# Sums of squares per tile on TensorE, the second memory kept in DRAM as two halves, one attention as a background job, longer lags in the odd layer

## The chip, the cores and the metric

The kernel is one program on one core of a Trainium2 chip. The metric is the device time of a launch in microseconds (us), lower is better. Almost all data is fp32; the large matrix products run on fp32r pairs (a value is kept as hi plus lo, and three products hi·hi, hi·lo, lo·hi are added).

## The reference, cut to what matters

One inference step of a two-layer decoder trunk, for 1024 prompt tokens and 8 sample tokens that share all weights.

```
for layer in (0, 1):
    mkv = rms_norm(mem_prompt, mem_norm[layer]) @ w_mem_kv[layer]      # memory keys and values, 256 rows
    h   = rms_norm(x, norm_pre[layer])
    mix = even_mixer(h, mkv, ...) if layer == 0 else odd_mixer(h, mkv, ...)
    x   = x + rms_norm(mix @ w_out, norm_post[layer])

def rms_norm(x, g):        return x * rsqrt(mean(x * x, -1) + EPS) * g
def memory_attend(q, kv):  p = softmax(q @ k * MEM_HD**-0.5);  return p @ v          # 4 heads
# even_mixer: gated DeltaNet (4 heads), dilated sliding-window attention (3 groups x 4 heads), memory attention (4 heads)
# odd_mixer : RG-LRU (8 tiles of 128 channels, in 4 blocks), memory attention (4 heads)
```

The sample tokens attend to cached keys and values instead, and the caches are copied out, shifted by one position.

## The kernel before, in words

Channels lie on the 128 partitions and tokens along the free axis, in three chunks of 352, 336 and 344 columns (the last 8 columns are the sample tokens). A projection (`proj`, `mm3`) makes one 128-channel tile: it loads 128 weight columns into one of 3 buffers (tag "w"), ScalarE casts them to hi, GpSimd takes lo (line 154), and TensorE runs 24 products for each chunk into one PSUM bank of the pool "p"; a drain on ScalarE or VectorE empties the bank. After each chunk `tick()` moves background jobs on by one step. A job is a generator in a named lane ("group", "combine", "cached", "norm0" ...); `yield n` makes it skip n-1 ticks. What a tick issues is placed behind the last instruction that each engine has so far. A planner then orders all instructions by simulated readiness, so the order on an engine is fixed when the program is built, and an engine that meets an instruction whose input is late waits.

Tiles of one tag share that tag's buffers. In the pool "me" the tags "qm", "gm" and "mm" have one buffer each: `mem_head` keeps a query in "qm", a gate in "gm" and the mix in "mm", and `swa_ahead` (line 517) takes the three in turn for projections that it makes ahead of their use.

The stages that the change touches, in order of time:

- Start (0 to 80 us). `mem_norm` and `x_rstd` call `chan_rstd` (209): 8 squares on ScalarE, VectorE adds each odd square to the even one before it (215), and `tok_rstd` (188) sums the four results over channels with matmuls against a column of ones (197), one group of accumulating products for each block of 128 tokens; then rsqrt on [128 x 3] values and a product that spreads the result. `mem_kv(0)` projects the first memory meanwhile.
- The DeltaNet stage around 290 to 370 us. VectorE inverts 32x32 triangles in a serial loop (746, 748) at high priority; `mem_head(0)` and three `swa_ahead` projections (keys (0,), (0,1,0), (0,0,0), in tiles pa0, pa010, pa000) fill TensorE. `mem_scaled` (295) multiplies the memory by its norm factors on GpSimd (302) and stores 1 MB to `memd` (303) on ScalarE's DMA queue.
- The end of the even layer (1075 to 1180 us). Head 3: `swa_gate(3)` (tile wb3), `mem_query` (wq03), `mem_gate` (wg03), then `mem_attend` (356) for head 3, then `mix_put` (1358) splits the 12 mix tiles into hi and lo for the output projection (tiles wo00, wo01 ...); the tile of head 7 comes from the job `combine` (1041), the tile 11 from the attention.
- Between the layers (1270 to 1400 us). `chain` (1442) normalises the output (po), adds the residual and calls `chan_rstd` for the next layer's norm (pr); `mem_reload` (305) loads `memd` through the "w" buffers and splits it (278 on ScalarE, 279 on VectorE) into the tags mb; `mem_kv(1)` projects it (mk10 to mv13).
- The odd layer (1400 to 1760 us). Projections, `recur` (the scan of the RG-LRU, mostly VectorE and ScalarE) and one job `mem_cached` for each head in the lane "cached". Such a job has two tiny matmuls on TensorE: mx (421) transposes a maximum, VectorE makes a row of it (423 to 427), my (430) spreads that row.

Of the kernel before, what the change touches and what calls it, by code (L numbers as in the profile page):

```python
# [15 lines left out]
P = 128  # L16
# [49 lines left out]
def body(ctx, tc, I, O):  # L66
# [34 lines left out]
    def ptile(name):  # L101
        return banks["a"].tile([P, 512], F32, name=name, tag="a")
# [85 lines left out]
    def tok_rstd(pool, sqs, n, scale, name, pt=None):  # L188

        nb = -(-n // P)  # L190
        pt = pt or ctile
        cols = pt(f"{name}c")
        x, y, t = (pool.tile([P, nb], F32, name=f"{name}{i}", tag=f"tr{i}{nb}", bufs=2) for i in "xyt")
        for b in range(nb):
            o = min(b * P, n - P)
            for k, sq in enumerate(sqs):
                T.matmul(cols[:, b:b + 1], sq[:, o:o + P], ones[:, 0:1], start=k == 0, stop=k == len(sqs) - 1)
        V.tensor_scalar(x, cols[:, :nb], scale, EPS, op0=ALU.mult, op1=ALU.add)
        rsqrt(y, x, t)
        dg = pool.tile([P, CW], F32, name=f"{name}d", tag="dg", bufs=1)  # L200
        for b in range(nb):
            o, w = b * P, min(P, n - b * P)
            V.tensor_scalar(dg[:, o:o + w], ident[:, P - w:], y[:, b:b + 1], None, op0=ALU.mult)
        yield 1
        bc = pt(f"{name}b")
        T.matmul(bc[:, :n], ones, dg[:, :n], start=True, stop=True)
        return bc[:, :n]

    def chan_rstd(pool, xc, n, name):
        sqs = []  # L210
        for k in range(8):
            sq = pool.tile([P, CW], F32, name=f"{name}sq{k}", tag=f"sq{k % 2}", bufs=1 if k % 2 else 4)
            S.activation(sq[:, :n], xc[k], AF.Square)
            if k % 2:
                V.tensor_tensor(sqs[-1][:, :n], sqs[-1][:, :n], sq[:, :n], ALU.add)
            else:
                sqs.append(sq)
        yield 1
        return (yield from tok_rstd(pool, sqs, n, 1.0 / 1024.0, name))
# [53 lines left out]
    memd = dr.tile([P, 8, 256], F32, name="memd")  # L273
# [21 lines left out]
    def mem_scaled(pool):  # L295

        rs = pool.tile([P, 512], F32, name="mrs1", tag="mpt", bufs=2)
        nc.sync.dma_start(out=rs[:, :256], in_=rsd)
        for i in range(2):
            t = pool.tile([P, 4, 256], F32, name=f"mss{i}", tag="pm", bufs=2)  # L300
            nc.sync.dma_start(out=t, in_=I["memT"][:, i * 4:i * 4 + 4])
            G.tensor_tensor(t, t, rs[:, None, :256].broadcast_to([P, 4, 256]), ALU.mult)
            nc.scalar.dma_start(out=memd[:, i * 4:i * 4 + 4], in_=t)

    def mem_reload(pool):
        o = []
        for i in range(2):
            mf = wp.tile([P, NT], F32, name=f"mrl{i}", tag="w")[:, :1024].rearrange("p (k t) -> p k t", k=4)
            nc.sync.dma_start(out=mf, in_=memd[:, i * 4:i * 4 + 4])
            for k in range(4):  # L310
                hi, lo = (pool.tile([P, CB], F32R, name=f"mr{j}{i}{k}", tag=f"mb{j}{i * 4 + k}")[:, :256] for j in "hl")
                mem_split(1, i * 4 + k, mf[:, k], hi, lo)
                o.append((hi, lo))
        return [o], None
# [41 lines left out]
    def mem_attend(pool, l, h, q, gate, mix, tags=("pm", "mpt"), ticks=False):  # L356
# [3 lines left out]
        for half in range(2):  # L360
            pr = pool.tile([P, 4, 256], F32, name=f"pm{l}{h}{half}", tag=tags[0], bufs=1 if l or tags[0] != "pm" else 2)
            for b2 in range(2):
# [12 lines left out]
                if ticks:  # L375
                    tick()
# [5 lines left out]
            po = ptile(f"mo{l}{h}{half}")  # L382
            for kb in range(2):
                pt = ptile(f"mt{l}{h}{half}{kb}")
                for b in range(4):
                    T.transpose(pt[:, b * P:(b + 1) * P], pr[:, b, kb * P:(kb + 1) * P], ident)  # L386
                st = pool.tile([P, 512], F32, name=f"mpt{l}{h}{half}{kb}", tag=tags[1], bufs=2)
                V.tensor_copy(st, pt)  # L388
                T.matmul(po, vt[:, kb, h, :], st, start=kb == 0, stop=kb == 1)  # L389
# [3 lines left out]
    def cached(pool, rows, pieces, nrow, gate, mix, name, kvb=3):  # L393
# [25 lines left out]
        yield 1  # L419
# [8 lines left out]
        yield 1  # L428
# [10 lines left out]
        yield 1  # L439
# [27 lines left out]
    def mem_cached(pool, l, h):  # L467
# [6 lines left out]
        def pieces():  # L474
# [3 lines left out]
                      gms[l][:, h, :], mixs[l][:, 8 + h, :], f"mc{l}{h}", 3 - l)  # L478
# [14 lines left out]
    def mem_branch(pool, l, h, gt, q):  # L493
        mix = pool.tile([P, 1024], F32, name=f"mm{l}{h}", tag="mm")
        mem_attend(pool, l, h, q, gt, mix)
# [475 lines left out]
    def even_swa(x, sh0, sxa, order):  # L971
        with ExitStack() as es:
# [165 lines left out]
            swa_gate(3, x, sp, gt)  # L1138
            qm = sp.tile([P, 1024], F32, name="qm03", tag="qkv", bufs=5)
            mem_query(0, 3, x, I["we"][59], qm)  # L1140
            gm = mem_gate(sp, 0, 3, x, I["we"][63], "qkv", 5)
            sh0.close()
            xa = mix_tiles(0, sxa)
            drain_lanes("cached", "group")
            mem_attend(sp, 0, 3, qm, gm, gm, tags=("spr", "spt"), ticks=True)
# [4 lines left out]
            drain_lanes("combine")  # L1150
            for k, t in ((7, last["acc"]), (11, gm)):
# [32 lines left out]
    def odd(x, sh1, eo, sxa, order):  # L1184
        with ExitStack() as es:
# [8 lines left out]
            def attend(h):  # L1194
                mem_attend(lp, 1, h, qs[h], gs[h], gs[h])
# [72 lines left out]
            def recur(n, m, wl):  # L1268
# [5 lines left out]
                for w, dst in ((0, tr), (1, tx)):  # L1274
                    ww = [wl[w * 4 + k * 2 + m] for k in range(2)]
                    for ci, (c0, nn) in enumerate(CH):
# [3 lines left out]
                                     bias=hb[:, w * 8 + ti:w * 8 + ti + 1])  # L1280

# [89 lines left out]
    def out_layer(l, xa, xa_stack, order, late, w0):  # L1371

        with ExitStack() as so:
# [69 lines left out]
            def chain(ci, xr):  # L1443
# [3 lines left out]
                rs = yield from tok_rstd(np_, [acc], n, 1.0 / 1024.0, f"po{l}{ci}", ptile if l else ctile)  # L1447
# [68 lines left out]
    order = [0, 1, 2, 3, 8, 9, 10, 4, 5, 6, 7, 11]  # L1516
# [121 lines left out]
```

## Time and profile before

| | us |
|---|---|
| three runs | 1931.64, 1936.73, 1922.24 |
| median | 1931.64 |
| the profiled execution, whole | 1922.29 |
| its span, first to last instruction | 1920.5 |

In the profile PE is TensorE's matmuls, PEld its weight loads, DVE VectorE, ACT ScalarE, POOL GpSimd, SP the engine that issues most loads. Busy time is a share of the span; "clock" is the granted TensorE clock, where 1.00 is 2.4 GHz and 0.50 is 1.2 GHz. The line of a row is the line of the kernel file. Matmul ends are modelled, so starts are the better guide.

### The profile page before, as it was taken

How to read it: one execution, taken by the hardware profiler on the slowest of the kernel's cores; microseconds unless marked ns; L12 is line 12 of the kernel's file. 1: busy time of each engine (PE TensorE's matmuls, PEld its weight loads, DVE VectorE, ACT ScalarE, POOL GpSimd, SP SyncE). 2: the span in 40 equal slices, each digit the busy share in tenths (PEclk: the TensorE clock that was granted, in tenths of full speed). 3: DMA queues.
4: the chain of work that ended last, by engine and by line, in shares of the span. 5: the costliest groups of instructions: out<-in, count | busy, mean ns of one | idle time of the engine just before them, and what ended most of it. 6: DMA issues, size and time to landing. Idle time of an engine off the chain costs nothing.

```text
span 1920.5 us, 29152 instructions
## 1 busy us (share of the span) xinstructions
PE 1787.9 (93%) x11341; PEld 1729.0 (90%) x11341; DVE 1090.9 (57%) x2302; ACT 715.8 (37%) x1610; POOL 550.3 (29%) x367
## 2 busy tenths in 40 slices
PE   7999998898999899999999988977899999989996
PEld 7799998898999899999999977967899999988996
DVE  6878758545633314434436475558765646657546
ACT  5355533122322334333333333324334333436432
POOL 3422223322111013323433402124442424330201
PEclk9999998898999999999999998978899999999998
DMA  8435455543434545555564445446634332223454
GB/s 290 179 133 196 178 166 188 202 142 108 148 132 166 190 157 173 189 183 174 187 212 162 135 130 154 130 136 215 249 135 154 121 123 87 83 74 122 145 193 139
DMA packets 160699, 306.26 MB, mean 159 GB/s; under 512 B 25073, under 2 KB 120497, under 8 KB 158641
## 3 DMA queue, kind: packets, MB, share of 16 engines
q1 hardware_dynamic: 67024, 222.47, 33.5%
q10 hardware_dynamic: 93536, 81.93, 13.3%
q8 instruction: 89, 1.46, 0.3%
q14 instruction: 50, 0.40, 0.1%
HBM read 254.05 MB, written 138.28 MB: 204 GB/s over the span
## 4 chain that ended last, share of the span: by engine, by line
PE 70%; DVE 14%; DMA 6%; ACT 3%; issue 3%; POOL 1%; ACTq 0%; SPq 0%; DVEq 0%; POOLq 0%
PE ss L1004 2%; PE so L1037 1%; DVE tm L746 1%; PE mo L389 1%; PE gz L869 1%; DVE y L1449 1%; PE ms L366 1%; PE gt L874 1%; PE st L1027 1%; DMA sc3k<-cache_swa 1%; DMA mf<-mixd 1%; DVE lacc L1291 1%; DMA sfb<-fd 1%; DMA gst<-state_gdn 1%; DVE xi L748 1%
## 5 line engine op out<-in xcount | busy, mean ns | idle before, releaser
L1006 DVE CUSTOM_DVE_ANT_0 spr<-ss,cs 128x128 f32<-128x128 f32 (+1 forms) x96 | 32.4, 349 | 89.4 <-PE ss L1004 89.2
L640 DVE SCALAR_TENSOR_TENSOR acc<-pre,vec,acc 128x1024 f32<-128x1024 f32 x36 | 49.2, 1366 | 13.4 <-ACT acc L638 13.2
L1013 ACT ACTIVATE spr<-spr,snm 128x128 f32<-128x128 f32 (+1 forms) x96 | 42.2, 441 | 35.8 <-DVE snm L1008 35.8
L1410 POOL COPY mg<-mixs 128x8 f32<-128x8 f32 x24 | 9.7, 402 | 146.7 <-DVE wo01al L154 43.0
L1450 POOL TENSOR_TENSOR y<-y,xr 128x352 f32<-128x352 f32 (+2 forms) x24 | 23.0, 963 | 98.2 <-DVE y L1449 97.7
L1395 DVE TENSOR_TENSOR ya<-ya,ysq 128x352 f32<-128x352 f32 (+2 forms) x42 | 25.8, 615 | 40.3 <-ACT ysq L1394 40.2
L372 ACT ACTIVATE pm<-ms,nm 128x256 f32<-128x256 f32 x64 | 29.8, 472 | 42.7 <-DVE nm L370 26.7
L1004 PE MATMUL ss<-sw,sw 128*128 128x128 f32 (+1 forms) x192 | 42.4, 322 | 2.4 <-DVE sml L1006 2.4
L389 PE MATMUL mo<-mpt,vt 128*128 128x512 f32 x64 | 35.1, 632 | 7.8 <-DVE mpt L388 4.6
L1249 DVE SCALAR_TENSOR_TENSOR lacc<-lpre,vec,lacc 128x1024 f32<-128x1024 f32 x24 | 39.5, 1644 | 0.3
L1037 PE MATMUL so<-spt,svt 128*128 128x128 f32 x280 | 38.2, 275 | 0.0
L388 DVE COPY mpt<-mt 128x512 f32<-128x512 f32 x32 | 22.0, 687 | 28.5 <-PE mt L386 28.5
L1037 PEld LDWEIGHTS so<-spt,svt 128*128 128x128 f32 x280 | 36.2, 191 | 0.0
L1004 PEld LDWEIGHTS ss<-sw,sw 128*128 128x128 f32 x192 | 31.2, 189 | 3.0 <-DVE sml L1006 2.6
L366 PE MATMUL ms<-kt,qm 128*128 128x256 f32 x128 | 32.8, 387 | 0.0
L910 DVE TENSOR_TENSOR guu<-guu,gsc 128x128 f32<-128x128 f32 x28 | 8.0, 286 | 43.3 <-PE gsc L909 43.3
L990 DVE COPY svt<-svp 128x512 f32<-128x512 f32 x24 | 15.5, 686 | 28.7 <-PE svp L989 24.3
L746 DVE TENSOR_TENSOR tm<-bl,xi 128x1 f32<-128x1 f32 (+30 forms) x31 | 28.2, 910 | 3.2 <-DMA bl<-aqd 2.7
L366 PEld LDWEIGHTS ms<-kt,qm 128*128 128x128 f32 x128 | 23.8, 195 | 5.9 <-issue 2.2
L1246 DVE TENSOR_SCALAR lacc<-lpre,vec 128x1024 f32<-128x1024 f32 x8 | 17.1, 2136 | 21.1 <-ACT lpre L1236 21.1
L1294 POOL COPY lhl<-lacc 128x1 f32<-128x1 f32 x8 | 3.6, 450 | 88.7 <-DVE lacc L1293 88.7
L1031 ACT COPY spt<-st 128x384 f32<-128x384 f32 (+2 forms) x48 | 22.4, 477 | 15.3 <-PE st L1027 15.1
(2144 smaller groups left out, 7364.7 us busy)
## 6 DMA issues: line engine op xcount, KB each, us to landing
o_sw3s<-cache_swa SPq DMA_DIRECT2D x64, 1023.5 KB
o_sw2s<-cache_swa SPq DMA_DIRECT2D x16, 1022.0 KB
gaq<-aqd ACTq DMA_DIRECT2D x20, 512.0 KB
mf<-mixd SPq DMA_DIRECT2D x19, 344.0 KB
sfb<-fd SPq DMA_DIRECT2D x12, 512.0 KB
aqd<-aq ACTq DMA_DIRECT2D x4, 1024.0 KB
o_sw3p<-sw SPq DMA_DIRECT2D x8, 512.0 KB
mixd<-lgt ACTq DMA_DIRECT2D x8, 512.0 KB
```

The source lines that it names most:

```text
L366: T.matmul(ps[:, b * 256:(b + 1) * 256], q[:, (b0 + b) * P:(b0 + b + 1) * P], kt[:, h, :], start=True, stop=True)
L372: S.activation(pr[:, b2 * 2 + b, :], ps[:, b * 256:(b + 1) * 256], AF.Exp, bias=nm[:, b0 + b:b0 + b + 1], scale=SC, accum_out=lt[:, b0 + b ...
L389: T.matmul(po, vt[:, kb, h, :], st, start=kb == 0, stop=kb == 1)
L640: V.scalar_tensor_tensor(acc, pre[:, j:j + 1024], vc("gconv", ti * 4 + j), acc, ALU.mult, ALU.add)
L746: V.tensor_tensor(t3, bl[:, 0:i, i][:, None, :].broadcast_to([P, i, i]), xi[:, 0:i, 0:i].rearrange("p j c -> p c j"), ALU.mult)
L1004: T.matmul(po, q[:, bb * P:(bb + 1) * P], k[:, k0:k0 + w], start=True, stop=True)
L1006: V.tensor_tensor_reduce(pr[:, bb, :w], po, mask, 1.0, NEG, ALU.add, ALU.max, accum_out=ml[:, 0, g, bb:bb + 1])
L1013: S.activation(pr[:, bb, :w], pr[:, bb, :w], AF.Exp, bias=nm[:, bb:bb + 1], scale=SC, accum_out=ml[:, 1, g, bb:bb + 1])
L1037: T.matmul(po[:, (bb % 4) * P:(bb % 4 + 1) * P], vt[:, kb, :], pt[:, o:o + P], start=st, stop=sp_)
L1249: V.scalar_tensor_tensor(acc[:, :1024], pre[:, j:j + 1024], vc("lconv", ti * 4 + j), acc[:, :1024], ALU.mult, ALU.add)
L1395: V.tensor_tensor(acc[:, :n], acc[:, :n], sq[:, :n], ALU.add)
L1450: (V if k % 2 else G).tensor_tensor(yk[k], yk[k], xr[k], ALU.add)
```

## The change

- `chan_rstd` adds nothing on VectorE. Each of the 8 squares goes to TensorE by itself (`tok_sums`): one product for each block of tokens, each into its own PSUM column; one `tensor_reduce` then adds 8 columns. There are two halves of four squares with a `yield` between them.
- `mem_scaled` also splits the second memory into hi and lo, 256 columns at a time, into tiles in the tags "qm" and "gm" of "me" (one buffer each), and stores both: four stores, 2 MB in all. `mem_reload` loads sixteen pieces of 128 KB straight into the mb tiles and splits nothing.
- `mem_attend` becomes a generator of five steps. At the end of the even layer gate and query of head 3 come first, the lane "group" is drained, the attention starts in a lane "attend", and `swa_gate(3)` is projected meanwhile. Tile 7 becomes the last of the output projection, after tile 11.
- `cached` takes a lag for three of its yields; it is 3 instead of 1 for the heads 0 to 2 of the odd layer. `recur` ticks twice.

```diff
+    def tok_sums(cols, sqs, n, k0, kk):
+        for k, sq in enumerate(sqs):
+            for b in range(-(-n // P)):
+                o = min(b * P, n - P)
+                c = b * kk + k0 + k
+                T.matmul(cols[:, c:c + 1], sq[:, o:o + P], ones[:, 0:1], start=True, stop=True)
-    def tok_rstd(pool, sqs, n, scale, name, pt=None):
+    def tok_rstd(pool, cols, n, scale, name, pt, kk=1):
...
-        for b in range(nb):
-            o = min(b * P, n - P)
-            for k, sq in enumerate(sqs):
-                T.matmul(cols[:, b:b + 1], sq[:, o:o + P], ones[:, 0:1], start=k == 0, stop=k == len(sqs) - 1)
-        V.tensor_scalar(x, cols[:, :nb], scale, EPS, op0=ALU.mult, op1=ALU.add)
+        c = cols[:, :nb * kk]
+        if kk > 1:
+            V.tensor_reduce(t, c.rearrange("p (b k) -> p b k", k=kk), axis=AX.X, op=ALU.add)
+            c = t
+        V.tensor_scalar(x, c, scale, EPS, op0=ALU.mult, op1=ALU.add)
...
-        for k in range(8):
-            sq = pool.tile([P, CW], F32, name=f"{name}sq{k}", tag=f"sq{k % 2}", bufs=1 if k % 2 else 4)
-            S.activation(sq[:, :n], xc[k], AF.Square)
-            if k % 2:
-                V.tensor_tensor(sqs[-1][:, :n], sqs[-1][:, :n], sq[:, :n], ALU.add)
-            else:
+        cols = ctile(f"{name}c")
+        for half in range(2):
+            sqs = []
+            for k in range(4):
+                sq = pool.tile([P, CW], F32, name=f"{name}sq{half}{k}", tag="sq", bufs=5)
+                S.activation(sq[:, :n], xc[half * 4 + k], AF.Square)
                 sqs.append(sq)
-        yield 1
-        return (yield from tok_rstd(pool, sqs, n, 1.0 / 1024.0, name))
+            yield 1
+            tok_sums(cols, sqs, n, half * 4, 8)
+        return (yield from tok_rstd(pool, cols, n, 1.0 / 1024.0, name, ctile, 8))
...
-    memd = dr.tile([P, 8, 256], F32, name="memd")
+    memd = dr.tile([2, P, 8, 256], F32, name="memd")
...
             G.tensor_tensor(t, t, rs[:, None, :256].broadcast_to([P, 4, 256]), ALU.mult)
-            nc.scalar.dma_start(out=memd[:, i * 4:i * 4 + 4], in_=t)
+            hl = [pool.tile([P, 4, 256], F32R, name=f"msh{i}{j}", tag=("qm", "gm")[j], bufs=1) for j in range(2)]
+            for k in range(4):
+                mem_split(1, i * 4 + k, t[:, k], hl[0][:, k], hl[1][:, k])
+            for j in range(2):
+                nc.scalar.dma_start(out=memd[j, :, i * 4:i * 4 + 4], in_=hl[j].bitcast(F32))
     def mem_reload(pool):
         o = []
-        for i in range(2):
-            mf = wp.tile([P, NT], F32, name=f"mrl{i}", tag="w")[:, :1024].rearrange("p (k t) -> p k t", k=4)
-            nc.sync.dma_start(out=mf, in_=memd[:, i * 4:i * 4 + 4])
-            for k in range(4):
-                hi, lo = (pool.tile([P, CB], F32R, name=f"mr{j}{i}{k}", tag=f"mb{j}{i * 4 + k}")[:, :256] for j in "hl")
-                mem_split(1, i * 4 + k, mf[:, k], hi, lo)
-                o.append((hi, lo))
+        for k in range(8):
+            t = [pool.tile([P, CB], F32R, name=f"mr{j}{k}", tag=f"mb{j}{k}")[:, :256] for j in "hl"]
+            for j in range(2):
+                nc.sync.dma_start(out=t[j].bitcast(F32), in_=memd[j, :, k])
+            o.append(tuple(t))
...
-    def mem_attend(pool, l, h, q, gate, mix, tags=("pm", "mpt"), ticks=False):
+    def mem_attend(pool, l, h, q, gate, mix, tags=("pm", "mpt")):
...
-            po = ptile(f"mo{l}{h}{half}")
+            yield 1
+            sts = []
...
-                T.matmul(po, vt[:, kb, h, :], st, start=kb == 0, stop=kb == 1)
+                sts.append(st)
+            yield 1
+            po = ptile(f"mo{l}{h}{half}")
+            for kb in range(2):
+                T.matmul(po, vt[:, kb, h, :], sts[kb], start=kb == 0, stop=kb == 1)
...
-    def cached(pool, rows, pieces, nrow, gate, mix, name, kvb=3):
+    def cached(pool, rows, pieces, nrow, gate, mix, name, kvb=3, lag=1):
...
-        yield 1
+        yield lag
         ps = ctile(f"{name}mx")
...
-        yield 1
+        yield lag
         ps = ctile(f"{name}my")
...
-        yield 1
+        yield lag
         po = ctile(f"{name}po")
...
-                      gms[l][:, h, :], mixs[l][:, 8 + h, :], f"mc{l}{h}", 3 - l)
+                      gms[l][:, h, :], mixs[l][:, 8 + h, :], f"mc{l}{h}", 3 - l, 3 if l and h < 3 else 1)
...
-            swa_gate(3, x, sp, gt)
+            gm = mem_gate(sp, 0, 3, x, I["we"][63], "qkv", 5)
             qm = sp.tile([P, 1024], F32, name="qm03", tag="qkv", bufs=5)
             mem_query(0, 3, x, I["we"][59], qm)
-            gm = mem_gate(sp, 0, 3, x, I["we"][63], "qkv", 5)
+            drain_lanes("group")
+            start("attend", mem_attend(sp, 0, 3, qm, gm, gm, tags=("spr", "spt")))
+            swa_gate(3, x, sp, gt)
...
-            drain_lanes("cached", "group")
-            mem_attend(sp, 0, 3, qm, gm, gm, tags=("spr", "spt"), ticks=True)
+            drain_lanes("cached")
...
-            drain_lanes("combine")
-            for k, t in ((7, last["acc"]), (11, gm)):
+            drain_lanes("attend", "combine")
+            for k, t in ((11, gm), (7, last["acc"])):
...
                         S.activation(dst[:, c0:c0 + nn], ps[:, :nn], AF.Tanh, scale=0.5,
                                      bias=hb[:, w * 8 + ti:w * 8 + ti + 1])
+                    tick()
```

## Rows read from the trace of the kernel before

**Rows 1.** The page: busy us of each engine, share of the span, instructions.
```profile
PE 1787.9 (93%) x11341; PEld 1729.0 (90%) x11341; DVE 1090.9 (57%) x2302; ACT 715.8 (37%) x1610; POOL 550.3 (29%) x367
```

**Rows 2.** Stretches: us, length, busy PE PEld DVE ACT POOL, clock, DMA share, GB/s.
```profile
1116.00:1160.50 44.50, 36.94 (x186) 30.20 (x184) 36.72 (x61) 17.14 (x37) 2.54 (x5) 0.92 0.43 142
...
1310.00:1374.50 64.50, 46.45 (x279) 43.29 (x278) 58.14 (x97) 31.07 (x62) 40.00 (x26) 0.82 0.69 235
...
1505.76:1521.10 15.34, 11.85 (x59) 11.87 (x60) 14.39 (x24) 3.62 (x8) 10.23 (x9) 0.78 0.28 103
...
1689.25:1700.22 10.97, 5.46 (x23) 5.46 (x24) 6.50 (x12) 3.65 (x7) 2.69 (x3) 0.69 0.58 179
```

**Rows 3.** Timeline of TensorE around the first my: start, duration, instruction, idle before.
```profile
1505.27 0.33 PE L164 MATMUL wgo2p<-h1h,wgo2l 128*128 128x352 f32 x1
1505.44 0.32 PE L162 MATMUL wgo2p<-h1h,wgo2h 128*128 128x352 f32 x1
1509.25 0.55 PE L430 MATMUL mc10my<-cs,mc10mq 1*128 1x1 f32 x2 [3.49 <-DVE lacc L1254]
...
1510.48 0.50 PE L162 MATMUL wgo2p<-h1h,wgo2h 128*128 128x352 f32 x1
1510.77 0.50 PE L163 MATMUL wgo2p<-h1l,wgo2h 128*128 128x352 f32 x1
```

**Rows 4.** Timeline of VectorE there: the row that my reads.
```profile
1508.89 0.21 DVE L427 COPY mc10mq<-mc10mr 1x128 f32<-1x128 f32 x1
```

**Rows 5.** The chain that ended last, 1148 to 1161 us: start, length, what.
```profile
1148.30 1.90 DVE snum L1099
1150.20 0.61 DVE mpt L388
...
1160.16 0.44 ACT y L1389
```

**Rows 6.** The sums of squares of x, chunk 1, and the adds: x count, ns min/median/max.
```profile
L197 PE MATMUL r01c<-cs,r01sq x24: 166/250/250, 38.8 to 41.3; 128*128 128x1 f32 x24
...
L215 DVE TENSOR_TENSOR r01sq<-r01sq,r01sq x4: 499/1176/2426, 28.1 to 37.0; 128x336 f32<-128x336 f32 x4
```

**Rows 7.** TensorE's timeline: the wait inside the start stage, and one behind tile pa010.
```profile
51.14 0.69 PE L343 MATMUL mvt<-cs,vf 128*128 128x128 f32 x2 [3.39 <-DVE vf L323]
...
326.20 0.43 PE L162 MATMUL ws000p<-h0h,ws000h 128*128 128x352 f32 x1 [3.78 <-ACT pa L511]
```

**Rows 8.** VectorE's timeline, 324 to 352 us: the last use of gm00, and the triangles' end.
```profile
324.29 0.68 DVE L390 TENSOR_TENSOR mm<-mo,gm 128x512 f32<-128x512 f32 x1
...
351.21 1.12 DVE L749 COPY xtt<-xi 128x1024 f32<-128x1024 f32 x1
```

**Rows 9.** Instructions by tile: two projections, mem_scaled's multiply (ns min/median/max, starts).
```profile
L164 PE MATMUL ws000p<-h0h,ws000l x24: 315/320/495, 326.6 to 340.0; 128*128 128x352 f32 x8, 128*128 128x336 f32 x8, 128*128 128x344 f32 x8
...
L164 PE MATMUL wq01p<-h0h,wq01l x24: 315/320/495, 347.8 to 360.1; 128*128 128x352 f32 x8, 128*128 128x336 f32 x8, 128*128 128x344 f32 x8
...
L302 POOL TENSOR_TENSOR mss<-mss,mrs x2: 2546/2879/3212, 317.7 to 320.2; 128x1024 f32<-128x1024 f32 x2
```

**Rows 10.** Transfers on the chain: a store of 512 KB, a load of 344 KB.
```profile
644.36 4.87 DMA mixd<-gz
...
1118.64 2.92 DMA mf<-mixd
```

**Rows 11.** The second memory: the split, its first and last projections, first to last start.
```profile
L279 DVE SCALAR_TENSOR_TENSOR mrl<-mrl,vec,mrh x8: 471/475/2565, 1315.1 to 1322.9; 128x256 fp32r<-128x256 f32 x8
L163 PEld LDWEIGHTS mk10p<-mrl,mk10h x8: 189/330/330, 1318.8 to 1325.9; 128*128 128x128 f32 x8
...
L163 PE MATMUL mv13p<-mrl,mv13h x8: 280/281/378, 1361.2 to 1366.6; 128*128 128x256 f32 x8
```

**Rows 12.** SP's timeline: the weights issued behind the two loads of the memory.
```profile
1313.97 0.33 SPq L146 DMA_DIRECT2D mk10f<-wmem  x1
...
1318.75 0.42 SPq L146 DMA_DIRECT2D mk11f<-wmem  x1
```

More of the change, by code (lines that the diff above doesn't have):

```diff
@@ L186, in at_once @@
                 return e.value
-    def tok_rstd(pool, sqs, n, scale, name, pt=None):
+    def tok_sums(cols, sqs, n, k0, kk):
[5 more added lines that the diff above has]
+    def tok_rstd(pool, cols, n, scale, name, pt, kk=1):
         nb = -(-n // P)
-        pt = pt or ctile
-        cols = pt(f"{name}c")
         x, y, t = (pool.tile([P, nb], F32, name=f"{name}{i}", tag=f"tr{i}{nb}", bufs=2) for i in "xyt")
-        for b in range(nb):
-            o = min(b * P, n - P)
-            for k, sq in enumerate(sqs):
-                T.matmul(cols[:, b:b + 1], sq[:, o:o + P], ones[:, 0:1], start=k == 0, stop=k == len(sqs) - 1)
-        V.tensor_scalar(x, cols[:, :nb], scale, EPS, op0=ALU.mult, op1=ALU.add)
+        c = cols[:, :nb * kk]
[3 more added lines that the diff above has]
+        V.tensor_scalar(x, c, scale, EPS, op0=ALU.mult, op1=ALU.add)
         rsqrt(y, x, t)
@@ L209, in chan_rstd @@
     def chan_rstd(pool, xc, n, name):
-        sqs = []
-        for k in range(8):
-            sq = pool.tile([P, CW], F32, name=f"{name}sq{k}", tag=f"sq{k % 2}", bufs=1 if k % 2 else 4)
-            S.activation(sq[:, :n], xc[k], AF.Square)
-            if k % 2:
-                V.tensor_tensor(sqs[-1][:, :n], sqs[-1][:, :n], sq[:, :n], ALU.add)
-            else:
+        cols = ctile(f"{name}c")
[4 more added lines that the diff above has]
+                S.activation(sq[:, :n], xc[half * 4 + k], AF.Square)
                 sqs.append(sq)
-        yield 1
-        return (yield from tok_rstd(pool, sqs, n, 1.0 / 1024.0, name))
+            yield 1
+            tok_sums(cols, sqs, n, half * 4, 8)
+        return (yield from tok_rstd(pool, cols, n, 1.0 / 1024.0, name, ctile, 8))
     def norm_split(pool, xc, n, gname, gi, rs, outs, name, hb=2):
@@ L374, in mem_attend @@
                                  accum_out=lt[:, b0 + b:b0 + b + 1])
-                if ticks:
-                    tick()
             hs = slice(half * 4, half * 4 + 4)
@@ L494, in mem_branch @@
         mix = pool.tile([P, 1024], F32, name=f"mm{l}{h}", tag="mm")
-        mem_attend(pool, l, h, q, gt, mix)
+        at_once(mem_attend(pool, l, h, q, gt, mix))
         nc.scalar.dma_start(out=mixd[l][:, 8 + h, :], in_=mix)
@@ L1194, in attend @@
             def attend(h):
-                mem_attend(lp, 1, h, qs[h], gs[h], gs[h])
+                at_once(mem_attend(lp, 1, h, qs[h], gs[h], gs[h]))
                 nc.scalar.dma_start(out=mixd[1][:, 8 + h, :], in_=gs[h])
@@ L1446, in chain @@
                 yk = [t[:, k, :n] for k in range(8)]
-                rs = yield from tok_rstd(np_, [acc], n, 1.0 / 1024.0, f"po{l}{ci}", ptile if l else ctile)
+                pt = ptile if l else ctile
+                cols = pt(f"po{l}{ci}c")
+                tok_sums(cols, [acc], n, 0, 1)
+                rs = yield from tok_rstd(np_, cols, n, 1.0 / 1024.0, f"po{l}{ci}", pt)
                 for k in range(8):
@@ L1515, in body @@
     even_gdn(h0, prep, sprep)
-    order = [0, 1, 2, 3, 8, 9, 10, 4, 5, 6, 7, 11]
+    order = [0, 1, 2, 3, 8, 9, 10, 4, 5, 6, 11, 7]
     sxa = ExitStack()
```

## The prediction

> **What bounds the kernel now.** I read the page's busy times first: TensorE (PE) is busy 1787.9 of 1920.5 us [rows 1]. No edit here takes any sizeable product away, so time can only come out of two places: stretches in which PE idles (132.6 us in all), and stretches in which its granted clock is lower. Second I read the table of stretches around the places that the diff touches. It shows four of interest: 1116 to 1160.5 us has PE 36.94 of 44.5 busy with VectorE (DVE) at 36.72; 1310 to 1374.5 has PE 46.45 of 64.5 at a clock of 0.82 with DVE at 58.14; two short ones in the odd layer have clocks of 0.78 and 0.69 [rows 2]. Third come the timelines, for what ended each idle time: what the reader is to see there is that PE waits for a small DVE result, and that after the wait it does not run at its old pace [rows 3, 4]. Last, the chain of waits at the end of the even layer, which runs through the last attention [rows 5], and the rows on which the costs rest [rows 6 to 12].
>
> The profiled execution took 1922.29 us, 9.35 under the median of 1931.64. The sum is made against 1922.3 and then carried over.
>
> **Odd layer, lag 3 and one tick more per tile: -16.** In heads 0 and 1 the tiny product my stands in PE's fixed order ahead of the row that it reads. For head 0 PE waits 3.49 us up to 1509.25; the row was copied at 1508.89 and ready at 1509.10 [rows 3, 4]. The wait names the DVE instruction lacc ahead of that copy: DVE was busy 14.39 of 15.34 us [rows 2], so the row is late because it queues. After the wait, products start 0.29 us apart, before it 0.17 [rows 3]; with the clock at 0.78 over the stretch this is the 1.2 GHz level for a part of it. So a wait costs twice. The stretch held 59 products in 15.34 us; at 0.17 each they need 10.0, so 5.3 are lost. Head 1 has the same pattern once more; head 2 waits ahead of mx, with 23 products in 10.97 us [rows 2], which need 3.9: 7.1 lost. Together 2 x 5.3 + 7.1 = 17.7.
>
> With lag 3 the products mx, my and po go two ticks later. A tick is one chunk, and a chunk is 24 products, 24 x 0.17 = 4.1 us. The added tick per scan tile makes ticks denser, so that I count my at one to two chunks of work later than now. PE came to it at 1509.25 - 3.49 = 1505.76; one chunk later is 1509.9, and the row has been there since 1509.10. The job grows from 9 yields to 9 + 3 x 2 = 15 waits of a tick, plus its pieces, and still ends inside its head's 19 to 24 ticks, by my count of the loops. What is late next is the DVE row itself if the planner again places it behind the scan's long instructions; for that I keep about 2 back: -16. Bounds: -18 (all) and -8 (one of the three comes back with its clock loss, and the others leave half a us each).
>
> **Even layer's last attention in the background: -10.** The combine's DVE sum snum ends at 1150.20. Then the chain runs through the attention alone: mpt, two products mo, and on to 1160.16, when the last output tile could be drained [rows 5]. That tail is 10.0 us. After, the attention starts once query, gate and group are done, with the 72 products of wb3 (72 x 0.17 = 12.2 us) as its cover, and the tail ends with tile 7 from the combine, not with tile 11. Cost of the cover: the attention's DVE and ScalarE work only moves. Draining "group" earlier moves nothing onto PE, since its products are the same. What is late next is the combine. If it starts as late as before, the gain is 10; if DVE (36.72 of 44.5 busy) is the bound, the attention's DVE work still has to pass ahead of it and half of the gain goes: -4. If the idle PE time of the stretch, 44.5 - 36.94 = 7.6, goes too with the clock lost with it (0.92 against 1, 3.6), it is -14 at best from the parts that overlap. I take -10, the row's own tail.
>
> **Second memory reloaded as hi and lo: -6.** Eight splits leave DVE, of which the longest held it 2.57 us and the others 0.475 [rows 11]: 5.9 us. The adds of `chan_rstd` leave it too (12 for the three chunks), 0.5 us each at the least [rows 6]: 6. So DVE's 58.14 of 64.5 [rows 2] falls by 12. The weight buffers are no longer held by the memory: the load of mk10f was issued at 1313.97 [rows 12], behind the first half's splits, and can go when the last projection ahead of it frees a buffer. The memory's projections lasted from 1315.1 (first lo) to 1366.6 [rows 11], with PE idle for 18 us of the stretch. Their own work is 8 tiles x 24 products; one lasts 0.28 [rows 11], and two overlap, as starts 0.17 apart at a length of 0.32 show [rows 3]: 192 x 0.14 = 27 us, so the idle time is not all theirs. Added: sixteen loads of 128 KB, 2 MB where 1 MB was; the stretch already moves 235 GB/s [rows 2], at which 2 MB take 9 us if they overlap. Added on PE: 24 more one-column products per chunk, 72 x 0.114 (next part) = 8.2 us, in the idle 18. DVE's 12 less sets at most what is gained: -14 with the clock; the added PE work and a later memory give +4. I take -6: 12 less, minus half of the 8.2 and a little for the loads.
>
> **Sums of squares at the start: +2.** 24 products started between 38.8 and 41.3, the last lasting 0.25: 2.75 us or 0.114 each [rows 6]; 24 more in each of three chunks of x are 8.2 us on PE. The memory's own norm has them too, but PE has nothing to do yet. Back come 12 adds of 0.5 or more on DVE [rows 6] and so a part of the 3.39 us that PE waits for DVE's vf at 51.14 [rows 7]; and the sums can start after the first half. I take 8.2 - 3.4 - 2.8 = +2, the 2.8 being a guess of half of the adds. Bounds: +6 (only a part of the wait comes back), -3 (the adds stood on the path in full: 8.2 - 3.4 - 8).
>
> **The split moved to 320 us: +8.** This is the part that costs. The halves take the tags "qm" and "gm", one buffer each. "gm" is held until the last use of the gate of head 0, 324.29 + 0.68 = 324.97 [rows 8]; the multiply feeding it ends before (320.2 + 3.2 = 323.4 at the latest) [rows 9]. Then in order: four lo splits on DVE at 0.48, between the steps of the triangles, about 330; a store of 512 KB at 4.87 [rows 10], 335; the buffer goes to the second half: four splits, 339; its store, 344. Only then may pa010, the next in "gm", be drained. PE waits for that drain already: 3.78 us up to 326.20 [rows 7]. It would wait to about 345. Behind the wait are ws000p, 326.2 to 340.3, and wq01p, which ended at 360.4 [rows 9]; the 7 us between the two belonged to other results, which need not shift. So ws000p runs 345 to 359, wq01p 359 to 372: 12 later, of which I let a third come back in the gaps behind: +8. A wait of 19 us in place of 3.8 also lowers the clock, which is in the 12 as the 0.49 that a product took there before [rows 9]. Bound below 0: the planner's slot order lets pa010 have "gm" before the halves. Bound above +38: the next part. On ScalarE's queue two more stores stand; eight casts move with the splits.
>
> **The rivals.**
>
> *The slot wait grows to +38.* Place: 322 to 396 us. The splits are placed at low priority on DVE; if the planner puts them behind the triangle loop, which ends at 351.21 + 1.12 = 352.3 [rows 8], it goes: lo 354.3, store 359.2, lo 361.1, store 366.0, drain 2.3 later (three chunks) 368, ws000p to 382, wq01p to 396 against 360.4: 35, and 3 for the clock. For it: DVE runs the triangles back to back. Against it: the gate's last use at 324.29 got in between two of their steps [rows 8]. Time 1905 + 30 = 1935, slower than before; it decides once the shift is over 8 + 27 = 35. Chance .13.
>
> *The odd-layer waits come back elsewhere.* Same DVE, same scan, only other ticks: DVE 14.39 of 15.34 [rows 2] speaks for it; that the row was ready 0.15 before my started [rows 3, 4] speaks against. Gain 5 in place of 16: 1916. Chance .13.
>
> *The attention stays the end of the even layer*, because its DVE work is placed behind the combine's. Gain 2 in place of 10: 1913. Chance .08.
>
> *No slot wait and a denser reload.* +2 in place of +8 and -12 in place of -6: 1893. Chance .13.
>
> *The sixteen loads go one after another.* A 344 KB load took 2.92 us [rows 10]; sixteen at that in a row from 1305 end at 1352, and with 27 us of projections the stretch ends at 1379 where the last projection stood at 1366.6 [rows 11]: 12 later instead of 6 earlier, 1923. Against it: loads on one queue overlap, or 235 GB/s would not be seen [rows 2]. Chance .05. The Trainium skill, page "DMA: Bandwidth & Descriptors", section "Bandwidth", speaks for this rival: it asks for transfers of 1 MiB or more and gives 0.95 us for 64 KB, 6.15 for 1 MB (loads that GpSimd issues). Between the two, an estimate for 128 KB is 1.3 us and for sixteen single ones 21; no row of before shows loads of 128 KB by themselves.
>
> **How the numbers follow.** The sum is -16 - 10 - 6 + 2 + 8 = -22: 1900.3 on the profiled execution's base, 1909.6 on the median's. I predict 1905, between the two. Chance of that case .48, its own range 1892 to 1918. All lower bounds together are -18 - 14 - 14 - 3 + 0 = -49, all upper ones -8 - 4 + 4 + 6 + 38 = +36; they hardly come together. The range 1882 to 1935 holds all rivals up to the slot wait's own time and leaves out about half of that case, the deeper end of the dense one and a tenth of the others: below .2. Within 1% is what a measurement here can barely tell from no change: 1912.3 to 1951. Faster by more: three quarters of the main case (.37), the dense one (.13), and a third of the odd-layer and attention ones (.08): .58. Slower by more: the slot wait with a share of the others lost as well, .1. Same: .32.
>
> **What the profile after would show.** Right: no wait ahead of my or mx between 1480 and 1720 and a clock near 1 there; no attention rows behind the last snum; mk10f issued 5 us or more sooner against its stage's start, no DVE split there; a wait of 15 to 20 us of PE behind pa010, with the second store's end as what ends it. Wrong: that wait over 30 us or absent; waits of 3 us in the odd layer at other tiny products; the sums' one-column products costing much other than 0.114 each; the reload landing over 15 us after its issue.

## The result, and the profile after

The changed kernel takes 1946.94 us (median of 10 runs, 1938.49 to 1949.48), the kernel before 1925.66 (10 runs): a ratio of 1.0098, 95% interval 1.0074 to 1.0122, some 19 us slower. Forecast were 1905 and a gain. The ratios here and below leave out two single slow executions, one of the kernel before (4425.61 us) and one of best (3270.89 us). The profiled execution has a span of 1936.7 against 1920.5.

To see where the time went I took a few tiles in both traces, the last product of each (of wo07 the first), and subtracted their times. The following table has these differences by stage, for the changed kernel and for the experiments told below (us, + is slower than before).

| kernel | start, to wb0 | wb0 to wq01 | wq01 to ws322 | ws322 to wo07 | wo07 to wx1 | wx1 to the end |
|---|---|---|---|---|---|---|
| changed | +11.9 | +31.7 | -16.3 | -6.8 | +8.0 | -12.2 |
| only_sums | +8.8 | +2.0 | -6.3 | -0.9 | +1.0 | -0.7 |
| only_split | +1.8 | +29.0 | -11.1 | +0.4 | +0.5 | -0.1 |
| only_attend | -1.3 | +6.5 | +0.1 | -5.9 | +2.9 | -2.6 |
| only_lag | +2.1 | +2.8 | +6.7 | +1.2 | +3.2 | -11.9 |
| own_slots | +10.5 | +4.5 | -1.1 | -5.6 | +8.1 | -12.9 |
| no_sums | +0.8 | +25.1 | -4.6 | -4.0 | -5.3 | -11.4 |
| attend_lag | -0.1 | +6.2 | +3.9 | -4.4 | +1.0 | -12.6 |
| sq8 | +13.0 | +27.1 | -5.0 | -4.6 | +8.6 | -9.9 |
| pr_old | +9.7 | +30.3 | -12.6 | -6.3 | -1.3 | -12.5 |
| start_old | +0.4 | +25.5 | -7.9 | -4.8 | -1.8 | -8.9 |
| best | +0.6 | +3.6 | +4.2 | -4.5 | -1.7 | -9.8 |
| gm_mm | +12.4 | +20.7 | -5.0 | -7.0 | +8.3 | -11.9 |
| memv_sp | +10.6 | +31.6 | -1.6 | -4.9 | 0.0 | -12.5 |
| no_bulk | +10.4 | +30.9 | -15.5 | -3.9 | -1.9 | -12.4 |

Each line is one execution, and executions drift: only_lag has the same order of instructions as before until the odd layer, and its profiled execution still lies 15.9 us behind there. A single entry of a few us says little, a column says much. Verdicts on whole kernels rest on the ratios of the timed runs.

**The wait for the buffers.** VectorE's timeline of the changed kernel, 342 to 348 us (start, length, instruction), and ScalarE's (with the idle time before and its releaser):

```profile
342.03 2.40 DVE L285 SCALAR_TENSOR_TENSOR msh<-mss,vec,msh 128x256 fp32r<-128x256 f32 x3
...
346.67 0.93 DVE L359 SCALAR_TENSOR_TENSOR pa<-sg0t,wb0p 128x352 f32<-128x352 f32 x2
```

```profile
339.33 0.46 ACTq L313 DMA_DIRECT2D memd<-msh  x1
...
344.46 0.34 ACTq L313 DMA_DIRECT2D memd<-msh  x1
...
347.22 0.46 ACT L357 ACTIVATE sg0t<-wb0p 128x344 f32<-128x344 f32 x1 [8.69 <-DVE pa L359]
```

The last splits end at 344.43, the last store goes out at 344.46, and pa0 (tag "qm") is drained at 346.67. What pa0's buffer held were the hi halves; their second store went out at 339.33 and had landed at 342.5, by the semaphore events of the trace (a semaphore is a counter on which a transfer reports its landing and for which an engine's queue can wait). From then on the drain stood in VectorE's fixed order, behind the rest of the splits, one step of the triangles and two updates of the DeltaNet state, with no idle time between them. Until it ran wb0p held its bank, and ws010p couldn't begin. TensorE's rows by tile, ws010p, and the two waits that follow, in ScalarE's timeline and in TensorE's:

```profile
L162 PE MATMUL ws010p<-h0h,ws010h x24: 313/319/498, 347.5 to 360.3; 128*128 128x352 f32 x8, 128*128 128x336 f32 x8, 128*128 128x344 f32 x8
```

```profile
387.32 0.44 ACT L519 COPY pa<-ws000p 128x336 f32<-128x336 f32 x1 [18.30 <-DMA gX<-xd]
```

```profile
388.01 0.66 PE L162 MATMUL wq01p<-h0h,wq01h 128*128 128x352 f32 x1 [15.68 <-DVE sqkv L525]
```

ws010p starts at 347.5; before, it had ended when ws000p began at 326.20 [rows 7]. ws000p follows, and its last drains now stand on ScalarE behind the issue of gX, which waits for the result of the triangles: PE waits 15.68 us more, until 388.01. wq01p starts 41 us later than before [rows 9].

**The sums at the start.** Two stretches of the changed kernel inside r01c (us, length, busy PE PEld DVE ACT POOL, clock, DMA share, GB/s), the products of both in TensorE's timeline, and the products of r02c by tile:

```profile
42.75:46.00 3.25, 3.25 (x32) 3.25 (x31) 3.25 (x4) 2.23 (x5) 3.25 (x2) 1.00 0.42 144
47.39:49.80 2.41, 2.41 (x13) 2.41 (x13) 2.12 (x5) 1.67 (x5) 1.01 (x2) 0.50 0.77 195
```

```profile
42.75 3.41 PE L194 MATMUL r01c<-cs,r01sq 128*128 128x1 f32 x30
...
47.39 2.56 PE L194 MATMUL r01c<-cs,r01sq 128*128 128x1 f32 x12
```

```profile
L194 PE MATMUL r02c<-cs,r02sq x48: 165/250/353, 63.7 to 73.4; 128*128 128x1 f32 x48
```

PE is busy from end to end in both stretches and between them, yet the clock goes from 1.00 to 0.50: the first 30 products take 3.41 us, 0.11 each, the last 12 take 2.56, 0.21 each. r00c and r02c go the same way (the last 18 of each take 3.83 us); in r02c a wait of 0.41 us and a few other products stand between the parts.

**The odd layer.** From the start of wgo1 to the end of wgo7 as one stretch, in the changed kernel and then in the one before; below, the first my and the mx of head 2 in TensorE's timeline of the changed kernel:

```profile
1465.64:1766.14 300.50, 293.41 (x1794) 283.17 (x1793) 189.97 (x275) 125.53 (x237) 108.39 (x72) 0.99 0.31 105
```

```profile
1437.20:1747.10 309.90, 297.44 (x1794) 287.35 (x1792) 187.81 (x273) 125.44 (x233) 107.55 (x72) 0.97 0.31 101
```

```profile
1540.07 0.38 PE L441 MATMUL mc10my<-cs,mc10mq 1*128 1x1 f32 x2
...
1710.37 0.37 PE L432 MATMUL mc12mx<-cs,mc12sm 128*1 128x128 f32 x1 [4.51 <-DVE mc12sm L429]
```

The stretch is 9.4 us shorter and its clock 0.99 instead of 0.97. The waits of heads 0 and 1 [rows 3] are gone. That of head 2 ahead of mx is still there, 4.51 us.

**Between the layers.** ScalarE's timeline of the changed kernel, TensorE's wait behind it, and the store on the chain:

```profile
1393.14 0.37 ACT L329 COPY vf<-mv12p 128x256 f32<-128x256 f32 x1
1403.37 0.34 ACTq L348 DMA_DIRECT2D o_memv<-vf  x1
1403.75 0.48 ACT L232 CAST h1h<-hn2hf 128x344 fp32r<-128x344 f32 x1 [10.24 <-DMA x1d<-y]
...
1405.08 0.36 ACT L329 COPY vf<-mv13p 128x256 f32<-128x256 f32 x1
```

```profile
1405.50 0.69 PE L351 MATMUL mvt<-cs,vf 128*128 128x128 f32 x2 [9.87 <-ACT vf L329]
```

```profile
1383.78 19.52 DMA x1d<-y
```

The small store o_memv has its input at 1393.5 and goes out at 1403.37, when x1d, issued at 1383.78, has landed: right ahead of it ScalarE's queue has a wait for semaphore 107, on which x1d reports its landing and on which this store is to report its own. A cast and the drain of mv13 stand behind it on ScalarE, and PE waits 9.87 us for that drain.

### The profile page after: what moved, and what is told of

The parts are those of the page before. It is cut to its first block, busy times and chain, and to the rows that moved or that the text cites. A ratio compares the mean times of both kernels' runs of the same rounds, so it can differ in the third digit from the quotient of the medians.

```text
span 1936.7 us, 29533 instructions
## 1 busy us (share of the span) xinstructions
PE 1800.4 (93%) x11501; PEld 1740.1 (90%) x11501; DVE 1073.4 (55%) x2281; ACT 714.2 (37%) x1610; POOL 547.0 (28%) x367
## 4 chain that ended last, share of the span: by engine, by line
PE 78%; DVE 11%; DMA 5%; issue 2%; ACT 2%; ACTq 1%; POOL 1%; SPq 0%; DVEq 0%; POOLq 0%
PE ss L1015 2%; PE so L1048 1%; PE mo L400 1%; PE ms L374 1%; DMA x1d<-y 1%; DVE tm L757 1%; PE gz L880 1%; PE st L1038 1%; PE gt L885 1%; DMA o_sw3s<-cache_swa 1%; PE lg L162 1%; PE gks L802 1%; PE lg L164 1%; PE lg L163 1%; DVE xi L759 1%
## 5 line engine op out<-in xcount | busy, mean ns | idle before, releaser
L1261 DVE SCALAR_TENSOR_TENSOR lacc<-lpre,vec,lacc 128x1024 f32<-128x1024 f32 x24 | 32.9, 1371 | 0.3
L1001 DVE COPY svt<-svp 128x512 f32<-128x512 f32 x24 | 15.5, 684 | 29.1 <-PE svp L1000 23.6
L1271 POOL TENSOR_TENSOR lxl<-lacc,lxh 128x1032 fp32r<-128x1032 f32 x8 | 22.4, 2797 | 30.6 <-ACT lxh L1270 25.3
L376 DVE TENSOR_REDUCE nm<-ms 128x2 f32<-128x512 f32 x32 | 21.7, 683 | 13.0 <-PE ms L374 12.9
L1426 DVE TENSOR_TENSOR mbl<-mg,mbh 128x344 fp32r<-128x344 f32 x24 | 17.5, 729 | 19.4 <-ACT mbh L1425 19.2
```

The source lines that it names most:

```text
L1261: V.scalar_tensor_tensor(acc[:, :1024], pre[:, j:j + 1024], vc("lconv", ti * 4 + j), acc[:, :1024], ALU.mult, ALU.add)
L1271: G.tensor_tensor(lo, acc, hi, ALU.subtract)
```

## Experiments

Each ratio is the time of a variant over that of the kernel before, measured beside it, with its 95% interval. Where one variant is said to be sooner than another, it is the difference of two such ratios, good to some 5 to 8 us. A "stage" is a column of the table above.

**The four parts, each alone on the kernel before.** The diff of each is its part of the change as shown above.

> The kernel before with the sums of squares alone changed (each square summed on TensorE, two halves, 5 square buffers). Theory A (the change's parts add up, as the two traces read): the last sums of x end 11.5 us later and every later tile with them, so +12 at 300 us and about +12 at the end, plus or minus 3 for the sums between the layers. Rival B (the later start is cover only for work that waits anyway): +12 at 100 us but under +4 at the end. Rival C: the sums also cause the loss between the layers; then +18 to +20 at the end and mv13p ends 18 or more later.

Ratio 1.0015 (0.9991 to 1.0038): 3 us at most likely, not separable from none. r02b ends 8.7 us late, where 12 were expected, and most of this delay is gone by the end: nearer to theory A at the start, rival B at the end.

> The kernel before with the second memory alone split early and reloaded as halves. Theory A: ws010p starts about 30 us later because pa0 waits for the buffer qm, about 34 lost at 440 us, some 15 of it left at 1075 us, and 8 more lost between the layers because the loads wait for the last product of wo07p: +20 to +24. Rival B (the slot wait is swallowed by the DeltaNet stage, which waits on other engines): +8 or less. Rival C (the loss between the layers comes from the sums, not from the reload): +12 to +15, and nothing lost between 1270 and 1410 us.

Ratio 1.0075 (1.0049 to 1.0100), +14: the whole loss is at wb0 to wq01, and nothing is lost between the layers. Rival C.

> The kernel before with the last memory attention of the even layer alone made a background job. Theory A: -7 (wo04p starts 7 us sooner), kept to the end. My forecast's term: -10. Rival: the combine becomes the end and only -2 is left.

Ratio 0.9990 (0.9967 to 1.0012), -2, not separable from none. Its stage is 5.9 shorter. From wb0 to wq01 its execution is 6.5 longer, and that of attend_lag 6.2: the generator puts both transposes ahead of the products in the earlier heads too, which changes the order of instructions there. Whether this is a price or drift (only_lag has +2.8 there with the old order) was not tested.

> The kernel before with the lags and the added tick of the odd layer alone. Theory A: -12 as between the two traces, wgo2p and wgo4p each end about 6 us sooner. My forecast's term: -16. Rival: the waits move to other small products, -5 or less.

Ratio 0.9957 (0.9929 to 0.9984), -8; the stage itself -11.9. Theory A for the stage.

The four ratios add up to +7 us, the changed kernel has +19. The half-widths of the four (4.3 to 5.3 us, added in squares) make about 10 of the sum, so the 12 between them are only just there. The table says where to look: between the layers, where the changed kernel loses 8 and each part alone about 3 at most.

**own_slots.** The halves keep out of "qm" and "gm":

```diff
-            hl = [pool.tile([P, 4, 256], F32R, name=f"msh{i}{j}", tag=("qm", "gm")[j], bufs=1) for j in range(2)]
...
+            for k in range(0, 4, 2):
+                hi = pool.tile([P, 2, 256], F32R, name=f"msh{i}{k}", tag="mpt", bufs=2)
+                for q in range(2):
+                    mem_split(1, i * 4 + k + q, t[:, k + q], hi[:, q], t[:, k + q].bitcast(F32R))
...
+            nc.scalar.dma_start(out=memd[1, :, i * 4:i * 4 + 4], in_=t)
```

> The changed kernel, but the hi halves of the second memory take the tag mpt in pieces of 512 columns and the lo halves overwrite the multiplied memory in place, so that pa0 and pa010 find qm and gm free. Theory A (the slot order is the loss of this stage): ws010p starts no more than 15 us behind before, wq01p ends some 12 to 15 behind instead of 43.6, and the end comes 12 to 18 sooner than in the changed kernel, about 1931. Rival (the eight lo splits themselves delay the triangles, and these set the stage): wq01p still 25 or more behind, the end less than 6 sooner.

Ratio 0.9996 (0.9977 to 1.0016), 20 sooner than the changed kernel: the loss of this stage is gone, with the same splits still on VectorE. TensorE's rows by tile:

```profile
L162 PE MATMUL ws010p<-h0h,ws010h x24: 311/318/642, 320.8 to 333.9; 128*128 128x352 f32 x8, 128*128 128x336 f32 x8, 128*128 128x344 f32 x8
```

ws010p starts at 320.8 instead of 347.5. So it is the buffers, not the work of the splits.

**gm_mm.** Only the tags change: `("qm", "gm")[j]` becomes `("gm", "mm")[j]`.

> The changed kernel with the halves in the tags gm and mm instead of qm and gm: pa0 finds its buffer free, pa010 and pa000 wait. Theory (what is lost is the place of ws010p: it can't run while wb0p's drain into pa0 holds its PSUM bank): ws010p starts within 8 us of the start in own_slots, about 321, the 14 us of its products are back under the wait, wq01p ends about 30 behind before instead of 43.6 and the end is 8 to 14 sooner than in the changed kernel. Rival (only the time at which the last buffer comes free counts): wq01p ends 40 or more behind, the end within 5.

Ratio 1.0070 (1.0045 to 1.0094), about 5 sooner than the changed kernel, which is not separable from none; 8 to 14 were expected. The stage is where the theory puts it: ws010p starts at 321.1, wq01p ends 33.1 behind instead of 43.6.

**no_sums, start_old, pr_old.** The old sums everywhere, at the start alone, between the layers alone; the rest as changed.

```diff
     def chan_rstd(pool, xc, n, name):
+        if name[0] != "p":
...
+                if k % 2:
+                    V.tensor_tensor(sqs[-1][:, :n], sqs[-1][:, :n], sq[:, :n], ALU.add)
...
```

(start_old; in pr_old the condition is `==`.)

> The changed kernel with the old sums of squares (adds on VectorE); split, attention and lag as changed. Theory A (parts add up): 3 sooner than the changed kernel, about 1944, as the sums alone cost 2 to 3. Theory B (sums and reload cost more together: the one-column products push the end of wo07p back, and the reloads wait for that end): 10 to 15 sooner, about 1933, with the shift at wx1p no larger than at wo03p.

Ratio 0.9983 (0.9968 to 0.9998): 22 sooner than the changed kernel, more than theory B asked. 11 are the start, 13 between the layers.

> The changed kernel with the old sums of squares at the start only (memory norm and x); new sums between the layers. Theory: r02b back at 68 to 71 us, that is 10 sooner than in the changed kernel, because the 18 last products of each 48 no longer run at half clock; +8 between the layers stays; the end 8 to 12 sooner, about 1937. Rival (the DeltaNet stage takes a later start back): the end less than 3 sooner.

Ratio 1.0006 (0.9977 to 1.0036), 18 sooner. The start's 11.5 are kept, but the +8 is gone too, with new sums between the layers: the theory is wrong there.

> The changed kernel with the old sums of squares between the layers only (pr); new sums at the start. Theory B (between the layers the one-column products push the end of wo07p back and the reloads, which wait for that end, carry it on): from the start of wo07p to the end of wx1p 0 to -5 against before instead of +8, and 8 to 13 sooner than the changed kernel, about 1936. Rival (the start is what the sums cost): less than 4 sooner, +8 still there.

Ratio 1.0044 (1.0020 to 1.0069), 10 sooner, and -1.3 between the layers.

**sq8.** `bufs=5` becomes `bufs=8` for the norms at the start.

> The changed kernel with 8 square buffers instead of 5 for the norms at the start, so that the second half's squares need not wait for the first half's sums. Theory A (that buffer wait delays the last sums of x): r02b starts some 6 to 8 us sooner than in the changed kernel; the end within 4 of it, since the DeltaNet stage took the later start back in only_sums. Rival (the 24 products more and their place behind mv03p set it): r02b less than 3 us sooner.

Ratio 1.0099 (1.0067 to 1.0132). The squares are all done early, the sums are as late as before the edit; sq8, ScalarE's rows by tile and two stretches:

```profile
L221 ACT ACTIVATE r02sq<-x x8: 472/473/493, 46.5 to 51.0; 128x344 f32<-128x344 f32 x8
```

```profile
65.90:68.80 2.90, 2.90 (x28) 2.84 (x26) 2.36 (x4) 1.42 (x2) 2.90 (x2) 0.98 1.35 507
69.40:73.10 3.70, 3.70 (x20) 3.70 (x20) 0.42 (x1) 0.00 (x0) 2.13 (x1) 0.50 1.29 455
```

My theory falls, the rival holds: the products themselves, the last of them at half clock, and their place behind mv03p. PE is busy without a gap in this r02c.

**memv_sp and no_bulk.** What was open by then was the +8, which the changed kernel, own_slots, sq8 and gm_mm have, and start_old has not. All four have PE's wait at mvt (6.3 to 10.1 us).

```diff
-            nc.scalar.dma_start(out=O["memv"][l, :, h, :], in_=vf)
+            (nc.sync if l else nc.scalar).dma_start(out=O["memv"][l, :, h, :], in_=vf)
```

no_bulk leaves the cache copies that go with the first six weight loads of the odd layer for later:

```diff
+                if owed[0]:
+                    owed[0] -= 1
+                    owed[1] += 1
+                else:
+                    for _ in range(2 if owed[1] and len(bulk) > 1 else 1):
...
```

> The changed kernel with the four stores of the second layer's memory values issued by SyncE instead of ScalarE. Theory A (ScalarE's order is the loss: drain and casts stand behind a store's issue that waits): PE no longer waits over 3 us at mvt, from the start of wo07p to the end of wx1p 0 to -3 against before instead of +8, the end 6 to 10 sooner than in the changed kernel, about 1938. Rival (the slow landing itself delays the cast into h1, which sets the stage): +6 or more stays.

Ratio 1.0059 (1.0036 to 1.0082), 7.5 sooner than the changed kernel; 0.0 in place of +8; the wait at mvt is 1.6, as theory A has it. But by the semaphore events x1d landed 8.5 us after its issue in this run, and the store's input was ready after 11.4: ScalarE would have had nothing to wait for either. So this run does not show that the order on ScalarE is the cause.

> The changed kernel with the first six cache copies of the odd layer skipped between the layers and made up two at a time with later weight loads. Theory B (the copies slow the store x1d): x1d lands within 12 us of its issue instead of 19.5, the wait at mvt is under 3 us and the end 5 to 9 sooner. Rival (the copies have no part in it): x1d still 18 us or more, the wait at mvt stays at 6 to 10.

Ratio 1.0044 (1.0025 to 1.0064), 10 sooner; -1.9; the wait is 1.3, and x1d landed 8.1 us after its issue, as theory B has it. But the edit also moved the semaphores: o_memv no longer carries that of x1d here. ScalarE's timeline of no_bulk:

```profile
1385.57 0.54 ACTq L1475 DMA_DIRECT2D x1d<-y  x1
...
1394.79 0.37 ACT L336 COPY vf<-mv12p 128x256 f32<-128x256 f32 x1
1395.18 0.34 ACTq L355 DMA_DIRECT2D o_memv<-vf  x1
```

o_memv goes out as soon as its input is there, 9.6 us after x1d.

What the four kernels with the loss have in common stands in their semaphore events: the third o_memv carries the semaphore of x1d, so ScalarE waits for x1d's landing, 19.5 to 20.7 us after its issue. In start_old the two share the semaphore as well, but x1d lands after 7.4 us, with the copies still there, and the store (10.1 us after x1d) finds it done. In pr_old x1d takes 15.4, but the stores behind it carry other semaphores, and this wait is absent. So the loss takes both, a late landing of x1d and a store behind it that waits for this landing with a drain behind it on ScalarE; but no run changed one of the two alone. What makes x1d late stays open. In the four a copy is issued within 1 us of it, in start_old and memv_sp the next one comes 2.5 to 2.9 us later; only_sums does not fit this, with 21.9 us to the landing and the next copy 3.4 us behind.

**attend_lag and best.** The two parts that gain; and these with the split as in own_slots and the old sums.

> The kernel before with the background attention and the lags alone. Theory A (parts add up): -9 to -10 against before, about 1915. Rival (the attention's gain is real but its own run hid it): -14 or more. Rival (they disturb each other): -4 or less.

Ratio 0.9926 (0.9901 to 0.9950), -14: the fastest of all, 33 us under the changed kernel. With the lags at -8 some 6 are left for the attention, as much as its stage shows.

> Old sums, split with the halves in mpt and in place (as in own_slots), background attention, lags. Theory: no slot wait, no loss at the start, between the layers -5 against before as in no_sums, attention -5, odd layer -12: -20 to -24 against before, about 1903; bounds 1898 and 1912. Rival (the split gives nothing by itself, as the only_split run suggests): about 1913, as attend_lag.

Ratio 0.9950 (0.9922 to 0.9978), -10, no better than attend_lag: the rival holds, and the split gives nothing by itself even without its wait.

## Why the prediction was wrong

**The split at 320 us: forecast +8, measured +32 in its stage (25 to 32 in eight kernels) and +14 at the end of only_split.** The step that failed is "Only then may pa010, the next in "gm", be drained". The time of release came near: in only_split, whose stage begins 1.8 late, the last store goes out at 338.94 and has landed at 341.5 (forecast were 339 and 344). In the changed kernel it goes out at 344.46 and has landed at 347.1, in a stage that begins 11.9 late; that this is near 344 too is chance. But the halves take "qm" as well, and pa0 comes before pa010: so not only ws000p and wq01p but ws010p stands behind the wait, 14 us of products that lay in front of it before. I named qm in the step and followed gm alone. gm_mm shows the share: with qm free the stage loses 20.7. The second thing missed is the queue of ScalarE: the last drain of ws000p, pushed behind the issue of gX, cost a wait of 15.68 more. The rival "+38" had about this size at wq01p, but not its reason: the splits did get in between the steps of the triangles, all before 344.5. Part of the loss came back later: from wq01 to ws322 the nine kernels with a wait on these buffers gained 8.8 on the mean (2 to 16), the six others lost 1.3 (-6 to +7). That the DeltaNet head waits for other engines there is my reading and was not tested.

**The start: forecast +2, measured +9 to +13 in the eight kernels with the new sums.** The mis-sized term is 8.2: I carried 0.114 us of a full-clock row [rows 6] to 48 products in a row. The second part of each run takes 0.21. r02c lasts 10 us in place of 2.7, and mv03p ahead of it ends 4.2 late. Counted in PE's timeline from the first product of r00c to the last of wb0, the sums take 20.4 us in place of 8.9, which is +11.5 for the 8.2; the other products, which the forecast left as they were, take 4.1 more, all of it up to the end of bap, whose first products follow each other at 0.29 us where later ones have 0.16. The credits (the wait at vf, the adds) came in part: r00c begins 1.8 sooner and PE idles 1.9 less, 3.7 of the 6.2. By the end only_sums keeps 3 of it, in the changed kernel more: start_old is 18 sooner, 10 of which lie between the layers.

**Between the layers: forecast -6, measured +8.** The reload by itself is not where it is lost: with the old sums there it makes +0.5, -5.3, -1.3 and -1.7 (only_split, no_sums, pr_old, best), at most a part of the gain that I saw in VectorE's work. The step that failed is the sentence that takes "half of the 8.2 and a little for the loads". The new products push the end of wo07p 10.1 us away from its start in only_sums (4.5 in only_split), and what was late next, a store's landing and the work behind it on ScalarE (the wait of 9.87 at mvt), I had not named. With the new sums and without that wait the stage has -1.8, -1.9 and 0.0. One reading was wrong as well: mk10f was not issued behind the first half's splits, which start at 1315.1, after it [rows 11, 12]; it went out when wo07bl had freed a weight buffer. The sixteen loads did not go one after another: they were issued from 1343.08 to 1350.41 and landed 2.4 to 4.3 us later each, and PE's first product with them stands at 1349.55, right behind the last one of wo07p at 1349.39. The Trainium skill, page "DMA: Bandwidth & Descriptors", section "Bandwidth", asks for transfers of 1 MiB or more; the price of smaller ones is not seen in this place, where PE never waited more than 0.4 us for a load of the memory.

**The last attention: forecast -10, measured -4 to -7 in twelve kernels.** Mechanism right, size off, and inside its bounds. The tail after the last sum is gone, but the combine became the end, as the step said: the last mix tile is split at 1182.07, right behind snum's product with the gate. I took the row's own tail; the lower bound, -4, was the closer value.

**The odd layer: forecast -16, measured -9 to -13 in twelve kernels.** Mechanism right for two of the three waits, 6 us each. The third, head 2's mx, stays at 4.51: lag 3 moves my by two ticks, but mx of that head falls into the third chunk of wgo6p as before. Of the 7.1 that I had counted for it 1 us came (the wait was 5.51); the other two gave 6.1 each, where I had 5.3.

**The sum.** In the profile +11.9 + 31.7 - 16.3 - 6.8 + 8.0 - 12.2 make +16.2 (before rounding), where the forecast had -22. Its sign hung on the buffers and on the products of the sums; the two parts that gain kept their sign. The rival that ended on the other side named the right place, with a chance of 0.13.

## What to carry to other kernels

When an edit puts a tile into a tag with one buffer, list every tile that comes after it in that tag, in each of the tags that it takes, and ask for each which bank its producer holds meanwhile; the time of release alone isn't the price. A duration read from a short run of small products doesn't carry over to a run twice as long: read the clock over the longer run before multiplying. Where a store's issue waits, look for the semaphore that it waits for, and for whose landing that is. Parts of a change that gain alone (here attention and lags, -14 together) are worth a run of their own before they go in with the others.

## What the runs showed of the hardware

A run of one-column fp32 products lost the full clock although PE was busy without a gap: 0.11 us each at 1.00 in the first part and 0.21 at 0.50 in the last, in r00c and r01c of the changed kernel and in r02c of sq8; the products behind it start at half clock too. A store of 1.4 MB (x1d, the one between 1367 and 1400 us) took 8.1 us to land with no DRAM copies beside it (no_bulk), and with them 7.4 (start_old) to 21.9 (only_sums). A later store that waits for the same semaphore stood 9.8 us on ScalarE in the changed kernel until that one had landed, and the work behind it with it.
